# A decoder step on one core: the second half of layer 0's FFN by seven block products in 19 of its slices, with weight sums added by VectorE in place

## The chip, the cores and the metric

One Trainium2 chip; the program runs on one of its cores. The metric is the device time of one execution in microseconds (us), smaller is better. A core has engines with instruction streams of their own: TensorE (PE; its weight loads are listed apart as PEld and overlap the matmuls), VectorE (DVE), ScalarE (ACT), GpSimd (POOL) and SyncE (SP, which here only starts transfers). They wait for each other by semaphores. Working tiles lie in SBUF, matmul results in eight banks of PSUM, and the weights come from device memory (HBM) by DMA queues that the engines feed: SyncE's carries nearly all loads and stores, POOL's the transfers that add to what they write.

## The reference

One inference step of a decoder of two layers, in float32, for 1024 prompt tokens and 8 sample tokens. Every layer has a mixer (layer 0 a gated linear recurrence with memory attention, layer 1 stick-breaking attention over one shared K/V with memory attention) and then a feed-forward network, the FFN:

```python
D_MODEL = 1024
D_FF = ((8 * D_MODEL + 3 * 256 - 1) // (3 * 256)) * 256

def swiglu(h, w_gu, w_down):
    gate, up = jnp.split(h @ w_gu, 2, axis=-1)
    return (jax.nn.silu(gate) * up) @ w_down
...
    for l in range(DEPTH):
        g = g_norm[l]
        hn = rmsnorm(h, g[0])
        if l < N_A:
            mix, S = a_mixer(hn, w_in_a[l], lbs[l], hg_norm[l], mem_k[l], mem_v[l], w_o[l], hg_s0[l])
        else:
            mix = b_mixer(hn, w_in_b[l - N_A], sb_bias[l - N_A], k_all, v_all, q_pos, k_pos,
                          mem_k[l], mem_v[l], w_o[l])
        h = h + rmsnorm(mix, g[1])
        h = h + rmsnorm(swiglu(rmsnorm(h, g[2]), w_gu[l], w_down[l]), g[3])
```

D_FF is 2816, that is 22 slices of 128.

## The kernel before, in words

**Tokens and number format.** The tokens are worked on in two groups: g = 0 has 512 prompt tokens, g = 1 the other 512 and the 8 sample tokens, 520 columns in two halves of h = 260. Activations lie transposed, features on the partitions, eight tiles of 128 features. Every float32 operand is split in two parts in the format fp32r: ScalarE casts (the high part), VectorE subtracts the high part from the source (the low part). A product of two such operands is three matmuls: high by high, high by low, low by high. `split_w` (lines 206 and 207) does this for plain weights: raw weights come by a SyncE load into a buffer, the two parts go to a tile `ws`. `split_to` (227, 228) does it for activations.

**The FFN, three forms of it.** A slice is 128 of the 2816 middle features: its gate and its up projection, silu(gate) times up, and the split of the result into a middle tile `m`. The 22 slices go in five parts, `PARTS = [(0, 5), (5, 5), (10, 4), (14, 4), (18, 4)]` (first slice, count). After the slices of a part its down projection adds to the residual tile R: eight output tiles, nf x 3 x 2 matmuls each.
- class `ffn` (697) is the plain form: `proj` (212, matmul line 220) takes 8 tiles of features x 3 x 2 halves of columns = 48 matmuls for the gate, as many for the up projection, into PSUM pair tiles `mm`. Here silu is made of exponentials (`silu`, 230: clamp at -44 by VectorE, exp, ln, exp by ScalarE, a multiply by VectorE), the functions that attention needs too, so it can be interleaved with attention.
- `gate_up_q` (452) does the same 96 matmuls into four single banks Q(0) to Q(3), called `q`, and calls meanwhile for a share of the activations' block sums (the argument `side`). Its gate is ScalarE's Silu.
- `gate_up_w` (482) is the block form. Gate and up weights are a 2 x 2 block matrix (gate or up by rows 0-511 or 512-1023), the activations a 2 x 2 block matrix too (those rows by the two column halves). Seven products of blocks and sums of blocks give all four result blocks where eight would be used directly: `product` (505, matmul line 511) is 4 x 3 = 12 matmuls, a slice 84. Four of the products take sums of weight blocks, four take sums of activation blocks, `y`, `z` and `u`, made by `sums_w` (279), which adds the two halves of a split activation to the full value (`full`, four adds of 260 columns per pair of feature tiles, line 298) and then does four differences and their splits. A product's accumulator in part starts from the negated copy of another one: lines 518 and 521 are ScalarE copies by -1 from one bank to the next.

The order of a slice's products, with their accumulators, is written out by hand:

```python
        product(pa, 0, True)
        nc.scalar.activation(pb[:, :h], pa[:, :h], AF.Copy, scale=-1.0)
        product(pd, 1, True)
        product(pb, 2)
        nc.scalar.activation(pc[:, :h], pb[:, :h], AF.Copy, scale=-1.0)
        product(pa, 3)
...
        product(pb, 4)
...
        product(pc, 5)
...
        product(pb, 6)
        act[0] = nc.scalar.activation(sg[:, h:n], gt[:, :h], AF.Silu)
```

pa, pb, pc and pd are the banks q0 to q3. pa holds the gate, pb (after its last product) the up projection of the first half of the columns, and both are read by the next instructions before the next slice may write the bank again.

**Weight sums.** `weight_sums` (549) makes the four block sums of the weights in device memory: for each part 16 transfers on POOL's queue, copies (line 568) and adding transfers (566), half the rows at a time, each held back by a small copy (563) until the work has come as far as `now`. It is called for layer 0, parts 3, 4 and 2 (`w0`, 48 transfers) and for layer 1, all parts (`ws`, 80), and its steps are interleaved with other stages. `gate_up_w` then loads seven blocks for a slice, three from the weights and four sums (`weight`, 494).

**Class `ffn_w`** (575) drives `gate_up_q` and `gate_up_w` for some parts: the first slices are plain (as many as the list `steps` has, while the activations' sums are made), the others go by blocks. It also says where tiles are taken from: `spl` (593) split weights, from the pool `wspl` of five or a second pool `cpool`, `raws` (605) raw weights, YT the sums y, z and u.

**The order of the work.** There is one instruction stream per engine, in program order: the driver at the end of the function calls generators, and `weave` takes steps from several in given proportions. Around the change it does: heads of layer 1 for g = 0 (`b0.heads`); `b0.sb` (stick-breaking attention, 1340) and `b0.mem` (memory attention, 864) interleaved with parts 0 and 1 of layer 0's FFN for g = 1, in the plain form; then parts 2 to 4 by `ffn_w`, three plain and nine block slices; the output projection of b0 (`o0`), in small steps with finishing work; K/V and heads for g = 1; the plain FFN of layer 1 for g = 0 beside the second attention; and at the end layer 1's FFN for g = 1 by `ffn_w`, three plain and 19 block slices. The attention outputs go into eight split tiles `xo` (`wo_tiles`, 310), which stay in SBUF until `o0.mm` reads them, through all of parts 2 to 4; these tiles come from the pool of tag `x0`.

In layer 0's FFN for g = 1 thus nine of 22 slices go by blocks, 13 plain.

Of the kernel before, what the change touches and what calls it, by code (L numbers as in the profile page):

```python
# [18 lines left out]
P = 128  # L19
# [4 lines left out]
def tile_decoder(  # L24
# [204 lines left out]

    def silu(dst, ps, g):  # L230
# [48 lines left out]
    def sums_w(g, xs, ops, YT, ZT):  # L279
# [5 lines left out]
        for k in range(4):  # L285
# [15 lines left out]
            b11, b12, b21, b22 = full(x0, 0), full(x0, h), full(x1, 0), full(x1, h)  # L301
# [150 lines left out]
    def gate_up_q(g, l, f, xt, side, n_side, first):  # L452
# [4 lines left out]
        for j in range(2):  # L457
# [14 lines left out]
            for a in range(2):  # L472
                d = sg[:, a * h : (a + 1) * h]
                if j == 0:
# [7 lines left out]
    def gate_up_w(g, l, f, ops, spl, raws):  # L482
# [5 lines left out]
        src = [  # L488
            (w_gu[l][0:512, gate : gate + P], 0), (sums[l][part][0][:, o : o + P], 4), (sums[l][part][1][:, o : o + P], 5),
            (w_gu[l][512:D, gate : gate + P], 1), (sums[l][part][2][:, o : o + P], 6), (sums[l][part][3][:, o : o + P], 2),  # L490
            (w_gu[l][512:D, up : up + P], 3),
        ]

        def weight(j):
            r = raws()
            nc.sync.dma_start(r, src[j][0].rearrange("(k p) m -> p k m", p=P))
            return r.rearrange("p k m -> p (k m)")

        def split(src):
# [3 lines left out]
            return w  # L503

        def product(ps, j, first=False):
            w = split(weight(j))
            i = src[j][1]
# [16 lines left out]
        nc.scalar.activation(sg[:, :h], pa[:, :h], AF.Silu)  # L524
        product(pb, 4)
        dt = T()
        nc.scalar.copy(dt[:, h:n], pd[:, :h])
        gt = T()
        nc.vector.tensor_add(gt[:, h:n], dt[:, h:n], pb[:, :h])
        product(pc, 5)  # L530
        nc.vector.tensor_sub(gt[:, :h], pc[:, :h], dt[:, h:n])
        product(pb, 6)
        act[0] = nc.scalar.activation(sg[:, h:n], gt[:, :h], AF.Silu)
# [41 lines left out]
    class ffn_w:  # L575


        def __init__(self, g, l, x, steps, first, rows, R=None, own=False):
# [3 lines left out]
            self.half = []  # L582

            def YT():
                if rows:
# [5 lines left out]
            self.sums = sums_w(g, x, self.ops, YT, YT if rows else lambda: A(F32R))  # L591

        def spl(self):
            self.n += 1
            if (self.pi or not self.rows) and not self.own and self.n % 8 in (1, 4, 6):
# [9 lines left out]
        def raws(self):  # L605
            self.r += 1
            if not self.rows and self.r % 2:
# [1029 lines left out]
```

## Time and profile before

| | us |
|---|---|
| runs | 2447.81, 2451.44, 2450.1 |
| median | 2450.1 |
| the profiled execution's own time | 2446.43 |
| its span in the profile | 2444.6 |

The profile is that of one execution. Its span goes from the first to the last instruction; the execution's own time is 1.8 us more. The view by stretches of time (windows) gives for each stretch the busy time of each engine with its count of instructions; the view of groups gives a row for each line and shape: count, busy time, mean nanoseconds of one, and after the second bar the idle time just before them with what ended it ("<-ACT q L521 0.4": 0.4 us that a write to q by ScalarE at line 521 ended). A row of the waits gives who waits, for what, and the total, the count and the longest. In the timeline a row is the start, the duration, the engine, the line and the operation, and at its end how many instructions it merges. `out<-in` are the tiles by the program's names, so `ws<-w,ws` is a weight split, `q<-x,ws` a matmul.

The page's 40 slices of the span show TensorE at nine tenths or more in nearly all of them, and its granted clock at nine tenths or more throughout (0.999 on average).

Where the stages lie, by the lines in the timeline: attention of layer 1 for g = 0 woven with parts 0 and 1 of layer 0's second FFN from 990 to 1209 us, parts 2 to 4 of it to 1428, finishing, K/V and heads to 1530, layer 1's first attention and FFN half to 2085 and its last FFN to the end.

### The profile page before, as it was taken

Reading aid. Unit: us, or ns where it says so; the run is one execution under the profiler, and the core shown is the slowest. Engines: PE = TensorE matmul, PEld = TensorE weight load, DVE = VectorE, ACT = ScalarE, POOL = GpSimd, SP = SyncE. Lnnn points to the kernel's source line nnn. Section 1 sums busy time; section 2 is a strip of 40 time slices with the busy share of each in tenths; the row PEclk is TensorE's granted clock in tenths of the full one; section 3 lists DMA queues with packets and bytes.
Section 4 is the critical chain, followed back from the end, with each engine's and each line's share of the span. In section 5 each row is a group of like instructions: output and inputs, shape, how many; then the busy total and the mean of one; then the engine's idle time right before and its main releaser. Section 6 shows DMA issues by size and latency. Waiting matters only on the chain.

```text
span 2444.6 us, 42106 instructions
## 1 busy us (share of the span) xinstructions
PE 2412.0 (99%) x15839; PEld 2159.3 (88%) x15839; DVE 1639.0 (67%) x2987; ACT 1251.2 (51%) x2441; POOL 186.1 (8%) x315
## 2 busy tenths in 40 slices
PE   8999999999999999999999999999999999999998
PEld 6888888888889988999999989877777888999998
DVE  5867557665897686654756686777788467755565
ACT  5547544344445555554434554555555445654445
POOL 1001101101000000111200102121000100000000
PEclk9999999999999999999999999999999999999999
DMA  5454666577746447677766649655354563464542
GB/s 187 120 166 117 161 191 158 134 192 186 209 132 172 123 156 232 179 179 168 196 166 165 202 139 293 196 151 150 99 163 121 145 192 119 140 193 144 148 145 73
DMA packets 534734, 397.42 MB, mean 163 GB/s; under 512 B 21325, under 2 KB 473018, under 8 KB 534530
## 3 DMA queue, kind: packets, MB, share of 16 engines
q1 hardware_dynamic: 505346, 315.02, 43.3%
q0 software_dynamic: 29184, 79.70, 14.1%
q8 instruction: 125, 2.05, 0.3%
q14 instruction: 79, 0.65, 0.1%
HBM read 364.81 MB, written 101.14 MB: 191 GB/s over the span
## 4 chain that ended last, share of the span: by engine, by line
PE 87%; DVE 6%; DMA 3%; issue 2%; ACT 2%; POOL 0%; SPq 0%; DVEq 0%; ACTq 0%; POOLq 0%
PE mm L220 46%; PE q L511 13%; PE q L648 9%; PE q L464 3%; PE mm L1042 2%; PE s L1188 1%; PE s L906 1%; PE s L1385 1%; PE mm L851 1%; PE mm L824 1%; PE s L875 1%; PE q L680 1%; PE s L1351 1%; DVE ws L207 1%; DMA b<-qd 1%
## 5 line engine op out<-in xcount | busy, mean ns | idle before, releaser
L220 PE MATMUL mm<-x,ws 128*128 128x260 f32 (+1 forms) x6240 | 1115.6, 335 | 3.5 <-DVE r L657 1.7
L220 PEld LDWEIGHTS mm<-x,ws 128*128 128x128 f32 x6240 | 941.0, 188 | 123.9 <-DVE x L228 2.1
L206 ACT CAST ws<-w 128x512 fp32r<-128x512 f32 (+1 forms) x652 | 382.3, 588 | 492.1 <-PE mm L220 336.2
L207 DVE TENSOR_TENSOR ws<-w,ws 128x512 fp32r<-128x512 f32 (+1 forms) x652 | 418.6, 648 | 246.0 <-ACT ws L206 232.0
L220 PE MATMUL mm<-m,ws 128*128 128x512 f32 (+1 forms) x1344 | 281.8, 361 | 0.5 <-DVE r L400 0.4
L220 PEld LDWEIGHTS mm<-m,ws 128*128 128x128 f32 x1344 | 217.8, 188 | 37.2 <-issue 1.0
L648 PE MATMUL q<-m,ws 128*128 128x260 f32 (+1 forms) x1824 | 222.0, 282 | 0.0
L648 PEld LDWEIGHTS q<-m,ws 128*128 128x128 f32 x1824 | 219.0, 188 | 1.3 <-DVE t L534 0.7
L502 DVE TENSOR_TENSOR ws<-w,ws 128x512 fp32r<-128x512 f32 x181 | 124.0, 690 | 89.7 <-ACT ws L501 86.3
L501 ACT CAST ws<-w 128x512 fp32r<-128x512 f32 x181 | 111.8, 621 | 110.8 <-PE q L648 31.9
L511 PE MATMUL q<-x,ws 128*128 128x260 f32 (+1 forms) x1188 | 158.1, 282 | 0.0
L511 PEld LDWEIGHTS q<-x,ws 128*128 128x128 f32 x1188 | 148.7, 188 | 0.0
L511 PE MATMUL q<-y,ws 128*128 128x260 f32 x912 | 119.7, 283 | 0.4 <-ACT q L521 0.4
L511 PEld LDWEIGHTS q<-y,ws 128*128 128x128 f32 x912 | 113.6, 188 | 0.9 <-ACT q L521 0.6
L464 PE MATMUL q<-x,ws 128*128 128x260 f32 (+1 forms) x720 | 91.3, 284 | 0.2 <-DVE r L400 0.2
L464 PEld LDWEIGHTS q<-x,ws 128*128 128x128 f32 x720 | 88.4, 188 | 1.8 <-DVE r L400 0.5
L511 PE MATMUL q<-a,ws 128*128 128x260 f32 (+1 forms) x672 | 87.0, 282 | 0.0
L511 PEld LDWEIGHTS q<-a,ws 128*128 128x128 f32 x672 | 83.2, 188 | 0.0
L657 DVE TENSOR_TENSOR r<-r,q 128x260 f32<-128x260 f32 (+1 forms) x128 | 48.4, 420 | 48.2 <-PE q L648 48.1
L237 DVE TENSOR_SCALAR t<-mm 128x512 f32<-128x512 f32 (+1 forms) x58 | 40.0, 690 | 48.6 <-PE mm L220 48.4
L563 POOL COPY mk<-a 128x1 f32<-128x1 f32 x36 | 21.9, 609 | 640.4 <-ACT a L1241 392.1
L566 POOL DMA_DIRECT2D wsum<-in_w_gu x64 | 58.5, 935 | 114.1 <-DMA wsum<-wsum 89.5
(355 smaller groups left out, 3027.8 us busy)
## 6 DMA issues: line engine op xcount, KB each, us to landing
w<-in_w_gu SPq DMA_DIRECT2D x297, 256.0 KB
w<-in_w_down SPq DMA_DIRECT2D x160, 256.0 KB
wsum<-in_w_gu POOLq DMA_DIRECT2D x72, 512.0 KB, 6.5
w<-wsum SPq DMA_DIRECT2D x104, 256.0 KB
w<-in_w_in_a SPq DMA_DIRECT2D x80, 256.0 KB
w<-in_w_o SPq DMA_DIRECT2D x64, 256.0 KB
wsum<-in_w_gu POOLq DMA_DIRECT2D x24, 640.0 KB, 6.8
wsum<-wsum POOLq DMA_DIRECT2D x24, 512.0 KB, 5.6
```

The source lines that it names most:

```text
L206: nc.scalar.copy(ws[:, 0, :n, :], raw[:, :n, :])
L207: nc.vector.tensor_sub(ws[:, 1, :n, :], raw[:, :n, :], ws[:, 0, :n, :].bitcast(F32))
L220: nc.tensor.matmul(ps[:, a, : PW[g]], wt, xt[k][:, xi, o : o + PW[g]], start=(k == 0 and wi == 0), stop=(k == nk - 1 and wi == 2),)
L237: nc.vector.tensor_scalar(sv(x, g), pv(ps, g), -44.0, None, op0=ALU.max)
L464: ins = nc.tensor.matmul(pp[a][:, :h], wt, xt[k][:, xi, a * h : (a + 1) * h], start=(k == 0 and wi == 0), stop=(k == ND - 1 and wi == 2),)
L501: nc.scalar.copy(w[:, 0, :], src)
L502: nc.vector.tensor_sub(w[:, 1, :], src, w[:, 0, :].bitcast(F32))
L511: nc.tensor.matmul(ps[:, :h], w[:, wj, k * P : (k + 1) * P], x[:, xi, :], start=(first and k == 0 and wi == 0), stop=(k == 3 and wi == 2), ...
L566: nc.gpsimd.dma_start(d, a, accum_op=ALU.add)
L648: nc.tensor.matmul(pp[a][:, :h], wt, mids[k][:, xi, a * h : (a + 1) * h], start=(k == 0 and wi == 0), stop=(k == nf - 1 and wi == 2),)
L657: nc.vector.tensor_add(d, d, pp[a][:, :h])
L1042: nc.tensor.matmul(pb[i][:, a, :], xt[k][:, xi, c * P : (c + 1) * P], ws[:, s, :], start=(k == 0 and wi == 0), stop=(k == ND - 1 and wi == 2),
```

## The change

- **Layer 0's FFN for g = 1** now goes wholly through `ffn_w` with the lists `steps` from part 0 on: three plain slices (`gate_up_q`) and 19 block slices. Parts 0 and 1 (the argument `beside`) are those beside attention. The four PSUM banks q are set up before them (`set_banks(True)`).
- **The gate beside attention** (`lean`): in these parts `gate_up_q` and `gate_up_w` make silu of a clamp, exp, ln, exp and a multiply, for both column halves at once after the last product, where the others call Silu.
- **Weight sums in place**: a part without sums in memory (`ready` is None) loads its four raw blocks at the slice's start, and VectorE adds: one sum to a new tile of the pool `npool`, three in place over raw blocks that aren't needed any more, each just ahead of its cast. This holds for parts 0 and 1 of layer 0 (seven slices) and all of layer 1 (19). `weight_sums(1, ...)` and all its interleaved steps are gone; `w0` stays, for parts 2 to 4 of layer 0. Part 2's three plain slices become block slices.
- **Tiles**: in parts 0 and 1 raw blocks come in turns from two tiles of `cpool` (`spare`) and the raw pool, split weights from the five of `wspl` alone; the activations' sums lie in tiles of tag `x0`, where `xo` was. `sums_w` is given the unsplit activations (`src=o1.R`), so `full` isn't called.
- **The attention output of g = 0** goes to device memory (`open(True)`, `put`: a copy out of PSUM by ScalarE and a SyncE store for each of the eight) and comes back by `load`: four SyncE loads spread over part 2, and eight splits interleaved with part 4's down projection.
- **The driver** runs parts 2 and 3 one step after the other with these, no longer through `weave` with weight sums.

```diff
+    def put(xo, i, cols, src):
+        if isinstance(xo, list):
+            split_to((xo[i][:, 0, cols], xo[i][:, 1, cols]), src)
+            return
+        t = B()[:, : cols.stop - cols.start]
+        nc.scalar.copy(t, src)
+        nc.sync.dma_start(xo[:, i, cols], t)
...
-            b11, b12, b21, b22 = full(x0, 0), full(x0, h), full(x1, 0), full(x1, h)
+            if src:
+                b11, b12, b21, b22 = (src[i][:, c : c + h] for i in (k, k + 4) for c in (0, h))
+            else:
+                b11, b12, b21, b22 = full(x0, 0), full(x0, h), full(x1, 0), full(x1, h)
...
+    def gated(d, x):
+        nc.scalar.activation(d, x, AF.Exp, scale=-1.0)
+        nc.scalar.activation(d, d, AF.Ln, bias=1.0)
+        nc.scalar.activation(d, d, AF.Exp, scale=-1.0)
+        nc.vector.tensor_mul(d, d, x)
...
-    def gate_up_w(g, l, f, ops, spl, raws):
+    def gate_up_w(g, l, f, ops, spl, raws, lean=False):
...
+        ready = sums.get(l, {}).get(part)
+
+        def load(W):
+            r = raws()
+            nc.sync.dma_start(r, W.rearrange("(k p) m -> p k m", p=P))
+            return r.rearrange("p k m -> p (k m)")
...
+        raw = {}
+        if not ready:
+            raw = {"a11": load(block(0, gate)), "a21": load(block(0, up))}
+            raw.update(a22=load(block(512, up)), a12=load(block(512, gate)))
 
         def weight(j):
...
+            if j == 1:
+                s1 = N()[:, :512]
+                nc.vector.tensor_add(s1, raw["a21"], raw["a22"])
+                return s1
+            if j == 2:
+                nc.vector.tensor_add(raw["a21"], raw["a11"], raw["a21"])
+                nc.vector.tensor_add(raw["a11"], raw["a21"], raw["a22"])
+            if j == 5:
+                nc.vector.tensor_add(raw["a11"], raw["a11"], raw["a12"])
+            return raw[("a11", "", "a11", "a12", "a21", "a11", "a22")[j]]
...
         product(pb, 4)
         dt = T()
-        nc.scalar.copy(dt[:, h:n], pd[:, :h])
...
+        if lean:
+            gt = dt
+            nc.scalar.copy(dt[:, :h], pd[:, :h])
+            nc.vector.tensor_add(gt[:, h:n], dt[:, :h], pb[:, :h])
+            product(pc, 5)
+            nc.vector.tensor_sub(sg[:, h:n], pc[:, :h], dt[:, :h])
+            nc.vector.tensor_scalar(sg[:, h:n], sg[:, h:n], -44.0, None, op0=ALU.max)
+            x, sg = sg, T()
+            product(pb, 6)
+            gated(sg[:, :n], x[:, :n])
...
         def raws(self):
             self.r += 1
-            if not self.rows and self.r % 2:
+            if self.pi in self.beside and self.r % 9 < 4:
+                return self.spare[self.r % 9 // 2][:, self.r % 9 % 2].rearrange("p (k m) -> p k m", k=4)
...
+        def load(self):
+            d, n, self.xo = self.xo, NG[self.g], []
+            ts = []
+            for k in range(0, ND, 2):
+                t = A()
+                nc.sync.dma_start(t[:, :, :n], d[:, k : k + 2, :n])
+                ts += [t[:, 0, :n], t[:, 1, :n]]
+                yield
+            for t in ts:
+                x = X(self.g)
+                split_to((x[:, 0, :n], x[:, 1, :n]), t)
+                self.xo.append(x)
+                yield
...
-    ws = weight_sums(1, range(5))
...
-    b0.open()
+    weave((b0.heads(), 8), (o1.finish(), 17))
+    b0.open(True)
+    set_banks(True)
+    fw = ffn_w(1, 0, o1.x, (5, 6, 5), 0, False, beside=(0, 1), src=o1.R)
+    weave((chain(b0.sb(), b0.mem()), 25), (chain(fw.part(0), fw.part(1)), 18))
+    p4 = fw.part(4)
+    back = b0.load()
+    drain(fw.part(2), islice(back, 4))
+    drain(fw.part(3), islice(p4, 4))
+    weave((p4, 4), (back, 8))
     f1 = ffn(1, 0, o1.x)
-    weave((chain(b0.sb(), b0.mem()), 25), (chain(f1.part(0), f1.part(1)), 18), (islice(ws, 34), 35))
-    set_banks(True)
-    fw = ffn_w(1, 0, o1.x, (5, 6, 5), 2, False, f1.R)
-    weave((chain(fw.part(2), fw.part(3), fw.part(4)), 24), (islice(ws, 8), 8))
-    f1.acc = fw.acc
+    f1.R, f1.acc = fw.R, fw.acc
```

More of the change, by code (lines that the diff above doesn't have):

```diff
@@ L502, in split @@
             nc.vector.tensor_sub(w[:, 1, :], src, w[:, 0, :].bitcast(F32))
[L503 to L507, printed above, removed]
+            i = (0, 4, 5, 1, 6, 2, 3)[j]
             for k in range(4):
@@ L575, in tile_decoder, with __init__ @@
     class ffn_w:
-        def __init__(self, g, l, x, steps, first, rows, R=None, own=False):
+        def __init__(self, g, l, x, steps, first, rows, R=None, own=False, beside=(), src=None):
             self.g, self.l, self.x, self.ops, self.steps, self.rows, self.own = g, l, x, [], steps, rows, own
@@ L582, in __init__ @@
             self.half = []
+            self.beside = beside
+            self.spare = [C() for _ in beside[:2]]
             def YT():
-                if rows:
+                if rows or beside:
                     return xpool.tile([P, 2, NG[1]], F32R, tag="x0", name=nm("y"))
@@ L625, in part @@
                     mids.append(
-                        gate_up_q(g, l, f0 + j, self.x, self.sums, self.steps[j], PARTS[self.first][0])
+                        gate_up_q(
+                            g, l, f0 + j, self.x, self.sums, self.steps[j], PARTS[self.first][0], pi in self.beside
+                        )
                     )
```

77 lines of the change are left out of this document (43 added, 34 removed).

## The prediction, made before the changed kernel was run

> **What bounds the kernel now.** The page comes first: the busy line and the chain that ended last.
>
> ```profile
> PE 2412.0 (99%) x15839; PEld 2159.3 (88%) x15839; DVE 1639.0 (67%) x2987; ACT 1251.2 (51%) x2441; POOL 186.1 (8%) x315
> PE 87%; DVE 6%; DMA 3%; issue 2%; ACT 2%; POOL 0%; SPq 0%; DVEq 0%; ACTq 0%; POOLq 0%
> ```
>
> TensorE is hardly ever idle, and the chain is 87% TensorE. An average says little of the stages that the change touches, so next comes the view by stretches: 990 to 1209 us is attention of layer 1 woven with parts 0 and 1 of layer 0's second FFN, 1209 to 1428 is its parts 2 to 4, 2085 to 2420 is nearly all of layer 1's last FFN.
>
> ```profile
> core 0: us, PE busy (x) PEld busy (x) DVE busy (x) ACT busy (x) POOL busy (x), PEclk, DMA share, GB/s
> 990.00:1209.00 219.00, 218.35 (x1691) 207.96 (x1691) 133.26 (x262) 113.52 (x230) 34.56 (x65) 1.00 0.70 174
> 1209.00:1428.00 219.00, 218.10 (x1723) 212.95 (x1722) 131.74 (x240) 104.11 (x198) 18.71 (x27) 1.00 0.64 179
> 2085.00:2420.00 335.00, 334.36 (x2775) 332.01 (x2774) 204.46 (x391) 175.55 (x366) 0.00 (x0) 1.00 0.51 147
> ```
>
> In all three TensorE is busy but for about 1 us, at full clock, and VectorE is 60% busy. The waits of TensorE in the first and in the third stretch are one row each:
>
> ```profile
> PE s L1380 <- ACT b L1374: 0.3, 1, 0.3
> ```
>
> ```profile
> PE q L511 <- ACT q L521: 0.4, 1, 0.4
> ```
>
> So every matmul taken away is time taken away, as long as the other engines still deliver its neighbours in time. What a block product costs is seen in the timeline of TensorE: twelve matmuls, and the next product starts 1.44 us later.
>
> ```profile
> 2185.39 1.60 PE L511 MATMUL q<-x,ws 128*128 128x260 f32 x12
> 2186.83 1.61 PE L511 MATMUL q<-y,ws 128*128 128x260 f32 x12
> ...
> 2191.16 1.11 PE L511 MATMUL q<-x,ws 128*128 128x260 f32 x8
> ```
>
> From 2185.39 to 2191.16 are four products, 5.77 us, or 0.120 us for a matmul. The plain projections run at the same pace:
>
> ```profile
> 1183.98 25.20 PE L220 MATMUL mm<-m,ws 128*128 128x260 f32 x208
> ```
>
> 25.20 / 208 is 0.121 us.
>
> **The gain.** A plain slice has 2 x 8 x 3 x 2 = 96 matmuls of 260 columns, a block slice 7 x 12 = 84. Nine of 22 slices were block slices, nineteen will be: 10 x 12 = 120 matmuls fewer, 120 x 0.120 = **14.4 us**. 84 of them leave the woven stretch (7 slices), 36 part 2.
>
> **VectorE's new load.** The costs of one instruction:
>
> ```profile
> L502 DVE TENSOR_TENSOR ws<-w,ws 128x512 fp32r<-128x512 f32 x181 | 124.0, 690 | 89.7 <-ACT ws L501 86.3
> L946 DVE TENSOR_TENSOR c<-c 128x512 f32<-128x512 f32 x24 | 16.2, 684 | 0.1
> L531 DVE TENSOR_TENSOR t<-q,t 128x260 f32<-128x260 f32 (+1 forms) x33 | 14.1, 427 | 3.3 <-PE q L511 1.9 <-issue 0.6
> ```
>
> L946 is an in-place add of 512 columns, which is what the change adds: four for each of 7 + 19 slices, 104 in all. What counts in a queue is the pitch from start to start, and that is shorter than the 0.69 of busy time:
>
> ```profile
> 2105.15 0.68 DVE L502 TENSOR_TENSOR ws<-w,ws 128x512 fp32r<-128x512 f32 x1
> 2105.75 0.69 DVE L228 TENSOR_TENSOR m<-t,m 128x520 fp32r<-128x520 f32 x1
> 2106.36 2.49 DVE L502 TENSOR_TENSOR ws<-w,ws 128x512 fp32r<-128x512 f32 x4
> ```
>
> 0.60 and 0.61 from one to the next; for 260 columns I take 0.34, as 0.427 less the same overlap. The Trainium skill says otherwise (VectorE: DVE Perf Modes, The DRAIN you can't avoid): the next operation does not start until the pipeline has emptied. By it each would count with its full 0.69. The four subtractions in 2.49 us do not agree.
>
> A layer-1 slice then holds VectorE for 7 splits and 4 adds x 0.61, 4 combinations x 0.34 and one 0.61: 6.71 + 1.36 + 0.61 = 8.7 us, beside 84 x 0.120 = 10.1 us of TensorE. That fits, and the order of instructions keeps the splits one whole slice ahead of their matmuls, so I cost the 76 adds of layer 1 at nothing; if that cover goes, see the second rival. In the woven stretch: 133 + 28 adds (17) + 21 more splits (13) + about 6 for the new gate steps - 16 sums no longer rebuilt (5) - 8 attention splits moved away (5) = 159 of some 209 us. That fits too.
>
> **Weight sums through memory.** 80 of the 128 transfers of line 566 and 568 go, and 3 of 7 SyncE loads in each layer-1 slice.
>
> ```profile
> q0 software_dynamic: 29184, 79.70, 14.1%
> w<-wsum SPq DMA_DIRECT2D x104, 256.0 KB
> ```
>
> The only TensorE wait on a DMA in the stretch after them, 1530 to 1930, is small, so the relief is worth 0, at most 0.7 us:
>
> ```profile
> PE s L1351 <- DMA a<-ksc: 0.7, 1, 0.7
> ```
>
> **Late gate in the woven slices.** Here the gate is exp, ln, exp instead of one Silu, so the last product's accumulator (q1) is read later, and the next slice's third product must wait for it.
>
> ```profile
> L238 ACT ACTIVATE t<-t 128x512 f32<-128x512 f32 (+1 forms) x42 | 26.6, 634 | 24.9 <-DVE t L237 22.7
> L241 DVE TENSOR_TENSOR t<-t,t 128x512 f32<-128x512 f32 (+1 forms) x42 | 29.0, 691 | 36.6 <-ACT t L240 36.2 <-issue 0.3
> L518 ACT ACTIVATE q<-q 128x260 f32<-128x260 f32 (+1 forms) x33 | 12.2, 371 | 9.0 <-PE q L511 8.2
> L886 ACT ACTIVATE b<-s,nmx 128x256 f32<-128x256 f32 x64 | 29.8, 470 | 17.9 <-DVE nmx L880 17.8
> L886 ACT ACTIVATION_READ_ACCUMULATOR b<-s,nmx 128x1 f32 x64 | 12.6, 197 | 0.0
> L875 PE MATMUL s<-c,a 128*128 128x256 f32 x32 | 8.4, 379 | 0.0
> ```
>
> From the end of the sixth product: subtract 0.43, a split queued between (0.61), clamp 0.43; three ScalarE passes 1.90, in some slices with a cast between; multiply 0.69 and multiply by q1 0.43: 4.5 us. On ScalarE stand, before the negated copy that opens the third product, also two score exponentials (2 x 0.67) and a cast (0.62): 0.43 + 0.61 + 0.43 + 1.90 + 1.33 + 0.62 + 0.37 = 5.7 us, or 6.2 with the extra cast. Cover: products 7, 1 and 2, 3 x 1.44 = 4.33, and two score matmuls of 8.4 / 32 = 0.26: 4.9. The wait is 0.8 to 1.4 by busy times; by pitches (0.08 less on each of some seven) 0.3 to 0.8, and none where more attention matmuls lie between. I take 0.4 at each of five slice-to-slice changes, 2.0 (0 to 7). Behind that copy ScalarE holds the next casts, five buffers deep, so nothing else goes late. At the two changes to the down projection the last middle tile (two more steps, cast 0.62, subtract 0.69) comes about 6 us after, against 1.44 + 24 x 0.120 + 1 = 5.3: 0.8 each, 1.6 (0 to 4).
>
> **First block slice of layer 1.** VectorE arrives there already full:
>
> ```profile
> 2088.00:2100.00 12.00, 12.00 (x100) 11.73 (x100) 11.99 (x27) 5.67 (x13) 0.00 (x0) 1.00 0.38 112
> ```
>
> That is the view by stretches again (VectorE 11.99 of 12). From the timelines of VectorE and of TensorE, the first split and the second product's first matmuls:
>
> ```profile
> 2102.35 0.68 DVE L502 TENSOR_TENSOR ws<-w,ws 128x512 fp32r<-128x512 f32 x1
> ```
>
> ```profile
> 2104.69 0.41 PE L511 MATMUL q<-y,ws 128*128 128x260 f32 x2
> ```
>
> The second split starts at 2105.15 (quoted above), when TensorE is already at that product. Two adds now stand before it and three more before the third: 1.2 and 1.8 us later, with transposes as part cover. I take 2.5 (0 to 5).
>
> **Attention output by way of memory.** Eight stores, four reloads on SyncE's queue, and 8 casts and 8 splits behind the last block slice. A reload waits for its two stores, and behind it stand raw weight loads; nine raw buffers at four a slice reach 2.2 slices, 22 us, ahead, so the queue costs 0. The splits lie beside 8 x 24 x 0.120 = 23 us of down projection, but three stand before the last middle tile: 1.0 (0 to 2).
>
> **Sum.** -14.4 + 2.0 + 1.6 + 2.5 + 1.0 = -7.3 on the profiled execution's 2446.4 us (span 2444.6 and 1.8 around it): 2439.1. The median shown lies 3.7 above that execution, so 2450.1 - 7.3 = **2442.8**.
>
> **Rivals.** (1) All is covered: 2450.1 - 14.4 = 2435.7, 2435 with the DMA relief. For: hardly a wait of TensorE in any stretch; against: the 4.5 us gate chain. (2) **VectorE falls behind in layer 1**, slower: three of seven products now follow an add on their own tile, and VectorE, in order, waits out the cast (0.62) between add and subtraction. With full busy times 11 x 0.69 + 4 x 0.43 + 0.70 = 10.0, plus 3 x 0.62 = 11.9 against 10.1. It decides once pitch and waits pass 10.1 a slice. Halfway, at 11.2, 19 slices lose 21; at each of five parts the down projection gives VectorE time without splits, I take 2.3 us (an estimate: 24 x 0.120 less one subtract and its overlap, 0.61), which gives back 11; with the sum above, 2442.8 + 10, and more where the slack isn't had: about 2456, at worst 2465. For: the 86.3 us that L502 already waits on L501; against: the pitch, and a slice of lead. The skill's DRAIN rule would be on this side. (3) The waits eat the gain: 7 + 4 + 3 is 14 of 14.4, 2449.5. The Trainium skill has a rule that leans there (Perfetto Trace Analysis, Identifying the Most-Contended Engine): judge TensorE by LDWEIGHTS, not by matmul busy time. In the woven stretch that is 208 of 219, 95%, against 99% in layer 1; if matmuls there were worth nothing, 36 x 0.120 = 4.3 would be left, 2445.8 before any wait. The 0.3 us of waits speak against it.
>
> **How the numbers follow.** Forecast 0.36, its own range 2438 to 2447; rival 1 0.18; rival 2 0.26; rival 3 0.20. Below 0.2%, 4.9 us, a measurement here can't tell it from no change. Faster: rival 1 and most of the forecast, 0.51; same: the rest of it and rival 3, less what falls outside, 0.21; slower: rival 2 and a little of 3, 0.28. For 8 in 10 the range goes from 2433 (rival 1 with the relief, and 2 for the median of a few runs, which lie 2447.8 to 2451.4) to 2460.
>
> **What would show it.** 15719 matmuls instead of 15839, and the woven stretch with parts 2 to 4 some 10 us shorter than 438: right on the gain. TensorE waits on the negated copy (ACT q) in the woven slices, up to 1 us each: right on the gate. One wait of 2 to 3 us at the first block slice of layer 1. VectorE at 75% in layer 1's FFN with TensorE at 99%: right on the adds; TensorE waiting there in every slice on DVE ws makes the prediction wrong, as would a woven stretch as long as before.

## The result, and the profile after

| | before | changed |
|---|---|---|
| median of the first runs, us | 2448.95 (4 runs) | 2435.39 (4 runs, 2434.12 to 2437.57) |
| median when both were run again | 2448.37 (21 runs) | 2434.73 (5 runs) |
| ratio, 95% interval | | 0.9947 [0.9934, 0.9959]; again 0.9945 [0.9931, 0.9958] |
| the profiled execution's span | 2444.6 | 2435.9; in the second profile 2433.0 |

The change makes the kernel 13.6 us faster, by the second interval 10.3 to 16.9. The time lies in the stated range and almost on the figure of the first rival (2435.7, all is covered), outside the forecast's own 2438 to 2447. The profile has to say whether that rival's story is true as well. The page of the changed kernel, busy engines and the queue of the sum transfers:

```profile
PE 2400.0 (99%) x15719; PEld 2145.9 (88%) x15719; DVE 1720.7 (71%) x3152; ACT 1278.1 (52%) x2518; POOL 95.9 (4%) x155
...
q0 software_dynamic: 12544, 33.56, 5.8%
```

120 matmuls fewer, VectorE 82 us more, POOL's queue down from 79.7 MB to 33.6. Busy time says nothing of where the span shrank. For that both traces are cut at the same events: the first scores of layer 1's attention, the first matmul of part 2, the first of the output projection behind part 4, and the first plain matmul of layer 1's last FFN. In the kernel before, these lie at 990.74, 1209.13, 1404.93 and 2066.66 us: parts 2 to 4 end at 1404.93, and what follows up to 1428 is already the output projection. The view by stretches of the kernel before (columns as in the prediction; the second number is the stretch's length):

```profile
990.74:1209.13 218.39, 217.74 (x1689) 207.52 (x1688) 133.26 (x262) 113.52 (x230) 34.56 (x65) 1.00 0.70 174
1209.13:1404.93 195.80, 194.91 (x1622) 194.19 (x1621) 114.56 (x213) 91.40 (x176) 18.71 (x27) 1.00 0.67 187
1404.93:2066.66 661.73, 652.74 (x3518) 538.52 (x3519) 473.19 (x751) 338.31 (x622) 64.19 (x88) 1.00 0.56 162
2066.66:2444.62 377.96, 370.42 (x3075) 367.10 (x3073) 234.55 (x453) 202.11 (x421) 0.00 (x0) 0.99 0.48 139
```

And of the changed kernel, in its second profile:

```profile
990.29:1203.73 213.44, 208.79 (x1605) 197.97 (x1604) 157.97 (x327) 129.60 (x284) 0.00 (x0) 1.00 0.36 108
1203.73:1395.59 191.86, 191.01 (x1587) 190.31 (x1585) 123.88 (x231) 100.70 (x196) 8.48 (x8) 1.00 0.54 161
1395.59:2055.27 659.68, 652.80 (x3518) 539.28 (x3519) 473.53 (x751) 338.24 (x622) 26.14 (x24) 1.00 0.45 137
2055.27:2433.02 377.75, 370.43 (x3075) 366.68 (x3073) 278.03 (x528) 202.27 (x422) 0.00 (x0) 0.99 0.34 99
```

Row by row: the woven stretch (attention interleaved with parts 0 and 1) -4.95 us with 84 matmuls fewer; parts 2 to 4 -3.94 with 35 fewer in the records; the stretch in which not a matmul was changed, -2.05; the last FFN -0.2 with 75 more instructions on VectorE. With 0.45 us earlier at the start that is 11.6. In the woven stretch TensorE was idle 0.65 us before and is idle 4.65 us now. Its waits there in the changed kernel's first profile:

```profile
PE q L552 <- ACT q L559: 1.9, 4, 0.6
PE s L1411 <- DVE b L1424: 1.1, 1, 1.1
PE s L1445 <- ACT b L1442: 0.5, 1, 0.5
PE s L1440 <- ACT b L1434: 0.5, 1, 0.5
```

So not all is covered. The first row is the late gate. The wait of 1.1 us is in no term and no rival of the prediction: attention's score matmul waits for VectorE. Its timeline in the second profile, where the same wait was 1.29 us, shows why:

```profile
1087.95 0.69 DVE L534 TENSOR_TENSOR n<-w,w 128x512 f32<-128x512 f32 x1 [1.12 <-DMA w<-in_w_gu]
1088.68 0.69 DVE L537 TENSOR_TENSOR w<-w,w 128x512 f32<-128x512 f32 x1
1089.29 0.28 DVE L207 TENSOR_TENSOR ws<-w,ws 128x128 fp32r<-128x128 f32 x1
1089.49 0.35 DVE L1422 TENSOR_SCALAR b<-s,biasp 128x128 f32<-128x128 f32 x1
1089.75 0.34 DVE L1424 SCALAR_TENSOR_TENSOR b<-s,biasp,cap 128x128 f32<-128x128 f32 x1
```

L534 and L537 are two of the new adds, for the first slice of part 1 (L534 writes a new tile, L537 adds in place). The first of them waits for its raw block, and attention's two instructions, which set a score bank free, stand behind it.

### The profile page after: what moved, and what is told of

Its sections match the earlier page's. It is cut to its first block, busy times and chain, and to the rows that moved or that the text cites. A ratio compares the mean times of both kernels' runs of the same rounds, so it can differ in the third digit from the quotient of the medians.

```text
span 2435.9 us, 41748 instructions
## 1 busy us (share of the span) xinstructions
PE 2400.0 (99%) x15719; PEld 2145.9 (88%) x15719; DVE 1720.7 (71%) x3152; ACT 1278.1 (52%) x2518; POOL 95.9 (4%) x155
## 4 chain that ended last, share of the span: by engine, by line
PE 83%; DVE 8%; DMA 3%; ACT 3%; issue 3%; POOL 0%; SPq 0%; DVEq 0%; ACTq 0%; POOLq 0%
PE mm L220 39%; PE q L552 16%; PE q L709 11%; PE mm L1102 2%; PE q L481 2%; PE s L1248 1%; PE s L1445 1%; DVE ws L207 1%; PE s L967 1%; PE mm L885 1%; PE mm L912 1%; PE q L741 1%; DMA w<-in_w_gu 1%; DMA c<-in_cache_mem_v 1%; PE s L936 1%
## 5 line engine op out<-in xcount | busy, mean ns | idle before, releaser
L220 PE MATMUL mm<-x,ws 128*128 128x512 f32 (+1 forms) x5280 | 991.3, 344 | 4.4 <-DVE r L718 1.6
L220 PEld LDWEIGHTS mm<-x,ws 128*128 128x128 f32 x5280 | 823.5, 188 | 124.5 <-issue 2.7
L206 ACT CAST ws<-w 128x512 fp32r<-128x512 f32 x612 | 357.6, 586 | 459.1 <-PE mm L220 288.5
L207 DVE TENSOR_TENSOR ws<-w,ws 128x512 fp32r<-128x512 f32 x612 | 392.2, 646 | 238.5 <-ACT ws L206 226.1
L709 PE MATMUL q<-m,ws 128*128 128x260 f32 (+1 forms) x2304 | 284.0, 283 | 0.6 <-DVE m L228 0.6
L709 PEld LDWEIGHTS q<-m,ws 128*128 128x128 f32 x2304 | 277.7, 188 | 2.9 <-DVE t L589 1.0
L552 PE MATMUL q<-y,ws 128*128 128x260 f32 x1824 | 243.0, 284 | 2.3 <-ACT q L559 1.9
L552 PEld LDWEIGHTS q<-y,ws 128*128 128x128 f32 x1824 | 228.1, 188 | 3.9 <-ACT q L559 2.7
L220 PE MATMUL mm<-m,ws 128*128 128x512 f32 x864 | 219.7, 402 | 0.1
L546 ACT CAST ws<-w 128x512 fp32r<-128x512 f32 x188 | 115.7, 622 | 96.2 <-PE q L552 42.2
L547 DVE TENSOR_TENSOR ws<-w,ws 128x512 fp32r<-128x512 f32 x188 | 128.9, 689 | 50.2 <-ACT ws L546 47.9
L227 ACT CAST m<-t 128x512 fp32r<-128x512 f32 (+1 forms) x88 | 54.9, 623 | 22.6 <-DVE t L777 11.9
L228 DVE TENSOR_TENSOR m<-t,m 128x512 fp32r<-128x512 f32 (+1 forms) x88 | 60.8, 691 | 7.7 <-ACT m L227 7.4
L275 DVE TENSOR_TENSOR st<-st,n 128x512 f32<-128x512 f32 (+1 forms) x91 | 62.2, 691 | 2.1 <-ACT n L274 1.3
```

The source lines that it names most:

```text
L206: nc.scalar.copy(ws[:, 0, :n, :], raw[:, :n, :])
L207: nc.vector.tensor_sub(ws[:, 1, :n, :], raw[:, :n, :], ws[:, 0, :n, :].bitcast(F32))
L220: nc.tensor.matmul(ps[:, a, : PW[g]], wt, xt[k][:, xi, o : o + PW[g]], start=(k == 0 and wi == 0), stop=(k == nk - 1 and wi == 2),)
L227: nc.scalar.copy(dst[0], src)
L228: nc.vector.tensor_sub(dst[1], src, dst[0].bitcast(F32))
L275: nc.vector.tensor_add(acc[:, :n], acc[:, :n], t[:, :n])
```

## The experiments

"Us by spans" below is from one profiled execution, the median from several; where they differ by 2 us both are given.

**Both kernels again** (no edit).

> The changed kernel once more, for its time against before and for a second profile. Theory A: the profiles are right, the change is worth what its stages add up to there: -5.3 us in the woven stretch, -4.0 in parts 2 to 4, about -2 after it once the 1.7 us of the half-clock stretch at 1688 us is taken off, +0.9 ahead of it, some -10.5 us in all. Rival B: the medians are right, -13.6 us, and the second profile shows a woven stretch nearer to -10, the waits there having been chance. Expected: a ratio of 0.9945 to 0.996 by A, 0.994 to 0.995 by B; the waits on the negated copy are there again by A, 4 of about 0.5 us.

Measured: 2434.73 us, 0.9945 [0.9931, 0.9958]. The four waits on the negated copy were there again (2.1 us), and the woven stretch was 213.44 after 213.06. The interval holds both theories' ratios; the stretches are A's.

> The kernel before against itself: its ratio should be 1.000 within 0.001 by both theories. Its second profile says how far a stage moves from one execution to the next. If the start of the woven stretch (the first scores of layer 1's attention, 990.7 us in the first profile) moves by about 1 us, then the 0.9 us that the changed kernel came later there is scatter and no part of the change; if it stays within 0.3 us, the change has cost it.

Measured: 0.9999 [0.9990, 1.0008]. The woven stretch was 218.39 again and parts 2 to 4 195.57 after 195.80: these stretches hardly move from one execution to the next, and differences of half a microsecond can be read in them. The start of the woven stretch was 990.57 here, and 991.68 and 990.29 in the changed kernel's two profiles, so the 0.9 us was scatter. Like the first profile of the changed kernel this one has a stretch at half clock (last section). The stretch in which no matmul was changed does move: it was 664.55 us here after 661.73, and only 1.7 of the 2.8 are half clock; in the changed kernel it was 661.11 (1.7 of it half clock) and 659.68. Pairs with the same clock differ by 11.6 us (2444.6 and 2433.0) and 10.9 (2446.8 and 2435.9), the medians by 13.6. Where the other 2 us are was not settled; by this second profile of before that stretch alone gained some 3 us in place of 2, and the interval reaches down to 10.3.

**Layer 1's sums by transfers again, layer 0 as changed.**

```diff
+    ws = weight_sums(1, range(5))
...
-    weave((chain(b0.sb(), b0.mem()), 25), (chain(fw.part(0), fw.part(1)), 18))
+    weave((chain(b0.sb(), b0.mem()), 25), (chain(fw.part(0), fw.part(1)), 18), (islice(ws, 34), 35))
...
-    weave((p4, 4), (back, 8))
+    weave((p4, 4), (back, 8), (islice(ws, 8), 8))
```

The other 38 of the 80 steps stand where they did before.

> The changed kernel with layer 1's weight sums made in memory by POOL's transfers again, as before, and loaded ready; layer 0 as changed. Theory A: the 76 adds on VectorE cost nothing, and the 80 transfers cost TensorE about 2 us of waits between 1405 and 1650 us: this run is 1 to 2 us slower than the changed kernel, about 0.996 of before. Rival (VectorE limits layer 1's last FFN a little): this run is 1 us or more faster than the changed kernel, with the stretch from the first block product of layer 1 to the end about 1 us shorter.

Measured: 2471.32 us, 1.0094 [1.0078, 1.0109]. Both theories fell: without the in-place sums of layer 1, the change to layer 0 makes the kernel 0.9% slower than before. The woven stretch, as a row of the view by stretches, and its first waits:

```profile
990.59:1226.09 235.50, 212.50 (x1605) 200.81 (x1604) 155.89 (x325) 129.14 (x284) 37.85 (x67) 0.97 0.73 186
```

```profile
PE s L1445 <- ACT b L1442: 7.2, 4, 3.4
PE q L552 <- DVE r L718: 6.1, 1, 6.1
PE s L1411 <- DVE b L1424: 5.3, 1, 5.3
```

22 us more than with the transfers gone, at a mean clock of 0.97 (the third number from the right). The engines named are not the cause; ScalarE's and VectorE's timelines show what they had waited for:

```profile
1223.67 0.62 ACT L546 CAST ws<-w 128x512 fp32r<-128x512 f32 x1 [9.44 <-DMA w<-in_w_gu]
```

```profile
1100.41 0.69 DVE L534 TENSOR_TENSOR n<-w,w 128x512 f32<-128x512 f32 x1 [5.10 <-DMA w<-in_w_gu]
```

It is the same add ahead of attention as above, with 5.10 us of waiting for its raw block in place of 1.12. Where they stood in the kernel before, beside plain slices of the same parts, the same 34 transfers cost nothing, as the next run shows.

**The kernel before with layer 1's adds alone.** `gate_up_w` as changed, `ws` and its steps taken out of the driver, the rest as before. Layer 1's raw blocks come in turns from two pools in part 0 too, where the kernel before used one; the second pool is another than in the changed kernel.

> The kernel before with only layer 1's weight sums moved to VectorE (four adds a slice, in place) and the 80 transfers gone; layer 0 as before. Theory A: 0 to -2 us against before (0.999 to 1.000). Rival: slower by 1 us or more (1.0005 and above). With the run before it, it says whether the two halves of the change add up.

Measured: 2445.56 us, 0.9987 [0.9978, 0.9996]. The woven stretch is 218.38, as with the transfers. The stretch up to the last FFN and the last FFN itself:

```profile
1405.56:2065.53 659.97, 652.41 (x3519) 538.55 (x3520) 473.71 (x751) 338.36 (x622) 26.14 (x24) 1.00 0.46 139
2065.53:2444.58 379.05, 371.08 (x3075) 367.34 (x3073) 277.95 (x528) 202.19 (x422) 0.00 (x0) 1.00 0.32 96
```

-1.8 us and +1.1 us against before. The 2 us that the changed kernel gains where no matmul was changed thus come from the transfers that are gone. The two halves of the change do not add: -2.8 us for this one by medians, +23 for the other, -13.6 together.

**The gate in halves.** The first half's gate is computed ahead of the sixth product, and the bank q1 is read right behind the last one:

```diff
+            x, sg = sg, T()
+            nc.vector.tensor_scalar(x[:, :h], pa[:, :h], -44.0, None, op0=ALU.max)
...
             nc.scalar.copy(dt[:, :h], pd[:, :h])
+            gated(sg[:, :h], x[:, :h])
...
             product(pb, 6)
-            gated(sg[:, :n], x[:, :n])
+            nc.vector.tensor_mul(sg[:, :h], sg[:, :h], pb[:, :h])
+            gated(sg[:, h:n], x[:, h:n])
```

> The changed kernel with the gate beside attention made in two halves: the first column half's exp, ln, exp and multiply stand ahead of the sixth product, and the last product's bank (q1) is read right behind that product, ahead of the second half's gate. Nothing is left out. Theory A (the wait on the negated copy comes from the gate's chain): the four waits, 2.0 us in all and some 2.7 us by the starts of the products, go, and the woven stretch, 213.1 and 213.4 us in the two profiles so far, becomes 210.5; some 0.9935 of before. Rival (ScalarE's queue, which gets three more instructions a slice, is what makes attention and products wait): the waits move to the scores and the stretch stays at 213 or grows.

Measured: 2432.99 us, 0.9933 [0.9920, 0.9947], the fastest of the runs that leave no sum out; its interval overlaps with that of the changed kernel. The row of the stretch:

```profile
992.27:1203.44 211.17, 208.31 (x1605) 197.81 (x1604) 157.28 (x334) 132.70 (x305) 0.00 (x0) 1.00 0.36 108
```

2.1 us shorter than the mean of the changed kernel's two, and no wait on the negated copy is left. The gate's chain has a part in that wait (theory A); the run without adds below shows that it isn't alone in it.

**The gate made longer.** In the lean branch of `gate_up_w`, ahead of `gated`:

```diff
+            for _ in range(2):
+                nc.scalar.activation(x[:, :n], x[:, :n], AF.Copy)
```

> The changed kernel with two more ScalarE passes over the 520 columns ahead of the exp in the gate of block slices beside attention; values unchanged. Theory A: each of five slice-to-slice changes waits 1.1 to 1.3 us longer, the two changes to the down projection up to as much, and the woven stretch goes from 213.3 to 219 to 222 us. Rival (the wait is set by something else): less than 2 us longer.

Measured: 2444.92 us, 0.9983 [0.9973, 0.9993]; the stretch 225.02 us at a mean clock of 0.98, that is about 220.5 at full clock (225.02 x 0.98, an estimate). The profile is that of the slowest of eight executions, 2450.85 us. The length is A's, the place is not: over the woven stretch and parts 2 to 4 the waits were

```profile
PE s L962 <- DVE b L955: 3.1, 3, 1.1
PE s L1442 <- ACT b L1436: 2.3, 3, 1.6
PE q L552 <- ACT q L559: 1.8, 2, 1.3
PE s L1447 <- ACT b L1444: 1.6, 2, 1.0
```

A longer gate is paid for mostly by attention's matmuls, whose ScalarE and VectorE steps stand behind it in the same queues.

**VectorE's slack in layer 1.** Each add accompanied by one more instruction of its size:

```diff
+                if l:
+                    nc.vector.tensor_tensor(s1, s1, s1, op=ALU.max)
                 return s1
```

and likewise for the three others.

> The changed kernel with every add of layer 1's weight sums accompanied by one more VectorE instruction of the same size on the same tile (a maximum of a tile with itself; values unchanged): 76 more. Theory A (VectorE has little slack in a block slice: 8.7 us of 10.1 by starts, 11.1 with these): it falls behind in the slices and recovers in the down projections, 5 to 12 us slower than the changed kernel, with TensorE waiting on VectorE's splits in the later slices of a part. Rival (the slack is larger than reckoned): under 2 us slower.

Measured: 2438.62 us, 0.9958 [0.9943, 0.9973]: 3.9 us slower than the changed kernel by medians, 3.6 by spans; between the two theories. The last FFN:

```profile
2056.28:2436.56 380.28, 371.57 (x3075) 367.05 (x3073) 316.46 (x604) 200.03 (x422) 0.00 (x0) 0.99 0.33 99
```

It is 2.5 us longer than 377.75, with VectorE at 316 of 380 us, and 2.1 of them are in part 0: its down projection starts 63.01 us after the stretch's first matmul, against 60.87 in the changed kernel. Of TensorE's waits there only the first block slices show one that matters:

```profile
PE q L560 <- ACT q L567: 1.6, 1, 1.6
```

No later slice waits for a split, so the queue of ready splits was never used up there.

**No adds in layer 1.** `weight` returns a raw block in place of each sum for layer 1.

> The changed kernel with layer 1's weight sums left out: the products take a raw block in place of each sum, so the 76 adds are gone and the output of layer 1 is another. Theory A: the adds cost next to nothing; the stretch from layer 1's first plain product to the last down projection, 341.8 and 341.3 us against 340.9 and 340.7 before, goes back to about 340.7, and the whole is 0 to 1 us faster than the changed kernel. Rival (the adds are paid for by waits that no row names): 2 us or more faster.

Measured: 2434.39 us, 0.9942 [0.9927, 0.9957]; by medians the changed kernel's time, by spans 1.8 us less, and the last FFN is

```profile
2054.98:2431.17 376.19, 369.53 (x3075) 366.48 (x3073) 235.41 (x454) 202.35 (x420) 0.00 (x0) 1.00 0.33 100
```

1.6 us below 377.75 (2.0 below the 378.20 of the first profile). The 76 adds cost 1.6 to 2.0 us, more than A said. By the starts of the down projections and of the parts behind them, 0.2 of the 1.6 lie in part 0, where the first block slice is, 0.9 in the five slices of part 1 and 0.5 in part 3's down projection. Without the adds the FFN is 1.8 us faster than before, and the number of loads is not the reason: in the run with layer 1's sums by transfers a slice has seven loads as before, and the same stretch took

```profile
2086.95:2463.50 376.55, 369.51 (x3075) 366.47 (x3073) 235.22 (x454) 202.05 (x420) 0.00 (x0) 0.99 0.48 139
```

**The transfers moved out of the woven stretch.** As two runs further up, with `(islice(ws, 34), 35)` in the `weave` of layer 1's first attention.

> As l1_by_dma (layer 0 as changed, layer 1's weight sums made by POOL's transfers), but the 34 steps of those transfers that stood in the woven stretch of layer 0 now stand in layer 1's first attention, woven with plain slices, where no block slice loads. Theory A (the transfers are dear only where in-place block slices load beside attention: 17 of the 20 us lost in l1_by_dma, with its half-clock stretches, lie in the woven stretch): the woven stretch is back at 213 to 214 us without waits on loads, and the whole is 2436 to 2445 us. Rival (the transfers are dear wherever they stand): still 2455 or more.

Measured: 2468.45 us, 1.0083 [1.0068, 1.0099]. The woven stretch is A's, 212.53 us without a wait on a load. The total is the rival's. From the output projection to the scores of the next attention 159.30 us passed where the kernel before took 148.67, with the DMA engines at 0.85, and TensorE's first waits there are

```profile
PE s L1411 <- DMA a<-ksc: 5.0, 1, 5.0
PE s L1375 <- ACT t L1370: 5.0, 2, 4.8
```

In both runs the eight steps that lay beside parts 2 to 4 before came bunched at the end of part 4, and these waits may be the price of that bunch; it was not tried apart. The larger loss lies behind them, in the attention with plain slices beside which the 34 transfers now stand. From its first scores to the last FFN, before and in this run:

```profile
1553.60:2066.66 513.06, 506.72 (x2506) 404.44 (x2507) 367.32 (x576) 262.24 (x488) 40.05 (x52) 1.00 0.50 145
1556.90:2090.47 533.57, 514.73 (x2507) 409.91 (x2507) 367.45 (x576) 261.38 (x487) 80.76 (x120) 0.98 0.63 173
```

That is 20.5 us more, where no block slice loads: the transfers are dear not only beside block slices, as A said. VectorE waits there for the loads of the sample tokens' queries:

```profile
DVE c L993 <- DMA b<-qd: 20.1, 10, 4.0
```

In the kernel before the same waits came to 2.2 us. Attention's steps stand behind them in VectorE's queue: after three of the longest, which ended at 1637.77, 1650.04 and 1787.98 us, TensorE waited 1.9, 2.9 and 3.7 us for VectorE and ScalarE. The attention of the woven stretch, beside which the transfers were free, has no sample tokens.

**No adds in layer 0's woven parts.** As for layer 1, for parts 0 and 1 of layer 0.

> The changed kernel with the 28 adds of weight sums in parts 0 and 1 of layer 0 left out: the products take a raw block in place of each sum, so the output is another. Theory A (the adds stand in VectorE's queue ahead of attention's steps on the score bank, and one of them waits for a load): the wait of the scores on VectorE at about 1090 us, 1.1 to 1.3 us in three profiles of the changed kernel, goes, and the woven stretch becomes 211 to 212 instead of 213.1 and 213.4. Rival (attention waits there because the products are fewer, whatever VectorE does): that wait and the stretch stay.

Measured: 2432.40 us (2 runs), 0.9936 [0.9918, 0.9954]. The stretch:

```profile
991.74:1201.32 209.58, 208.44 (x1605) 197.95 (x1604) 141.94 (x300) 130.05 (x283) 0.00 (x0) 1.00 0.36 108
```

3.5 to 3.9 us shorter, better than expected: the scores' wait at 1090 us is gone, and so is the wait on the negated copy, which A had not said. That wait thus needs both, the gate's chain and the adds. In the changed kernel's second profile ScalarE idled for an add, and the gate's first pass came behind (in the first profile the same idle time, 1.99 us, is put down to a matmul):

```profile
1113.16 1.14 ACT L546 CAST ws<-w 128x512 fp32r<-128x512 f32 x2 [2.20 <-DVE w L538]
1114.74 0.64 ACT L464 ACTIVATE t<-t 128x520 f32<-128x520 f32 x1 [0.44 <-DVE t L577]
```

**All sums on VectorE, on top of the gate in halves.** `w0` and its steps taken out.

> The gate in halves, and in addition the weight sums of layer 0's parts 2, 3 and 4 made by VectorE too, for both groups: no transfers on POOL's queue for sums are left. Theory A (a transfer taken away relieves TensorE where it stood, and the block slices of parts 2 to 4 have VectorE to spare): up to 2 us faster than the gate in halves alone, 2430 to 2433. Rival (parts 3 and 4 of the first group run beside attention with raw tiles from a pool that attention uses): 2 us or more slower, with waits of attention or of the products in the stretch before 750 us.

Measured: 2437.64 us, 0.9956 [0.9942, 0.9969], 4.6 us slower than the gate in halves by medians, 2.8 by spans. The stretch before, which the rival named, is not longer beyond scatter (the woven stretch starts at 992.45, with the gate in halves at 992.27). Parts 2 to 4 take 193.81 us against 191.88, and the relief that A hoped for does not show. Both were wrong about the place.

**Two of four adds on GpSimd, on top of the gate in halves.**

```diff
-                nc.vector.tensor_add(s1, raw["a21"], raw["a22"])
+                (nc.vector if l else nc.gpsimd).tensor_add(s1, raw["a21"], raw["a22"])
```

and the next add likewise.

> The gate in halves, and in parts 0 and 1 of layer 0 the first two of a slice's four adds made by GpSimd, which has nothing to do there; the other two stay on VectorE. Theory A (without its 28 adds the woven stretch was 209.6 us against 213.1 and 213.4, so VectorE's queue is what is left of the loss there): with 14 adds off VectorE the stretch becomes 209.5 to 210.5 instead of 211.2, and the whole is about 1 us faster than the gate in halves alone, some 2432. Rival (an add of 512 columns takes GpSimd several times the 0.69 us of VectorE, for which no row of this case has a price, and the second and third product wait for it, or VectorE's own instructions beside it get longer): the stretch becomes 213 us or more.

Measured: 2438.71 us, 0.9964 [0.9951, 0.9978]; the woven stretch is 216.00. The rival is right. Groups of GpSimd, and of VectorE's splits beside them:

```profile
L537 POOL TENSOR_TENSOR w<-w,w 128x512 f32<-128x512 f32 x3 | 4.2, 1392 | 0.2
...
L534 POOL TENSOR_TENSOR n<-c,c 128x512 f32<-128x512 f32 x1 | 2.1, 2069 | 21.9 <-DVE b L1434 21.9
```

```profile
L547 DVE TENSOR_TENSOR ws<-c,ws 128x512 fp32r<-128x512 f32 x19 | 14.5, 762 | 4.9 <-ACT ws L546 4.8
```

An add takes GpSimd 1.3 to 2.1 us by its groups in this stretch, and 19 of VectorE's splits have gone from 688 to 762 ns in the mean. The Trainium skill (GPSIMD Engine Reference, 4.1 Engine selection) puts elementwise work with two inputs at about twice VectorE's time there; 1392 against 690 ns agrees; the add of 2069 ns took three times as long.

## Why the prediction was right or wrong

The sign and the range were right; the sum, -7.3, was 4 us short of what the spans give (-11.6) and 6 short of the medians. Its base, 2450.1, was the median of three executions and 1.7 above the later one of 21; on that one the forecast would have been 2441.1 and the first rival 2434.0. By its own steps:

- **The gain, -14.4.** 15719 matmuls, as said. The share of parts 2 to 4 was 4.3 and came nearly whole (-3.9). Of the 10.1 in the woven stretch 8.8 came in the run without adds there (218.39 to 209.58), 5.0 to 5.3 in the changed kernel.
- **Late gate, +2.0.** Right in place and number: four waits of 0.5 us on the negated copy, 1.9 and 2.1 in all; with the gate in halves they are gone and 2.1 us with them. The mechanism was half of it, and the size is in part luck: the working left out the adds, which hold back the casts that stand ahead of the gate's passes, and in the run without adds the gate's chain alone makes no such wait.
- **Two changes to the down projection, +1.6.** Wrong: the matmuls of L709 show no wait in the woven stretch.
- **VectorE in the woven stretch, costed at nothing.** This step failed on the bad side. The count, 159 of 209 us, was right (158), but an engine with a quarter of its time free still works in order. The 28 adds and what waits behind them cost 3.5 to 3.9 us, some 2 of which are the gate's wait.
- **First block slice of layer 1, +2.5, and the other adds there at 0.** The mechanism was misplaced. TensorE has only small waits there (its own transposes lie between the products), 0.2 us of loss, while the 76 adds together cost 1.6 to 2.0, most of it in the part behind. Only with twice the adds did 2.1 us come at the first part. The last FFN still came out at -0.2 and +0.2: without the adds it is 1.8 faster than before. Why is open: it is not the loads, since with seven a slice it was 1.4 faster too. Part 0's raw blocks also come from another choice of tiles than before, which was not tried apart.
- **Reload of the attention output, +1.0.** Some 0.4 (4.3 less 3.9), or 0.7 if the 0.3 that parts 2 to 4 gained from the missing transfers alone (195.50 after 195.80) is added.
- **Relief from the transfers, 0, at most 0.7.** This term was mis-sized most: 2.05 us by the spans (some 3 by the second profiles), 1.8 in the run that took nothing else out of this stretch. The bound came from the one wait named DMA, that of L1351 on `ksc`, 0.7 and 1.0 us in the two profiles of before and 0.2 to 0.4 or none without the transfers. But waits on ScalarE went too: those of the matmuls of L1315 from 0.6 and 1.2 us to 0.2, and those of L1380 (L1440 in the changed kernel) from 2.1 and 1.6 to 1.1 and 1.0. With L1385 (L1445), 1.9 and 2.9 before and 2.1 and 1.9 after, the four rows come to 5.3 and 6.7 us before and 3.7 and 3.3 after, which is about the relief.
- **Rivals.** The time is the first one's, its condition does not hold: TensorE's idle time in the woven stretch rose by 4 us, and the relief and 2 us not settled filled the gap. The second, VectorE falling behind in layer 1, did not happen, and not even with 76 more instructions there beyond a few us. (Its price was also too high by its own figures: halfway between 10.0 and 11.9 is 10.95, not 11.2; 19 slices then lose 16 us, 5 after what the down projections give back, and the time is some 2448.) The third, waits that eat the gain, came true by half in the woven stretch (5 of 10.1) and nowhere else.

What the prediction did not see at all is that the two halves hang together: it costed the transfers by the trace of a stage in which they were free, and the change put block slices there, beside which the same transfers cost 22 us. Block slices are not the only such place: beside the sample tokens' attention and plain slices the 34 transfers came with a loss of 20.5. Common to both is an engine that waits, in order, for a load; that this is the whole reason was not tried apart.

## What to carry to other kernels

When a change makes a stage's loads more urgent, what else uses the DMA engines there must be priced against the new stage: a transfer that is free in one stage can be the bound in another, and moving it to a third that looks free can cost as much again. Free time on an in-order engine is not cover for an instruction that waits for a load; see what stands behind it, and read a bank that others wait for before a long gate, not after it. Two parts of a change can be worth -2.8 and +23 us alone and -13.6 together, so try each part alone before crediting either.

## What the runs showed of the hardware

A wait of TensorE can cost more than its length. In the changed kernel's first profile TensorE waited 1.92 us up to 1675.99; the granted clock (the third number from the right) in the microseconds after it:

```profile
1676.00:1677.00 1.00, 1.00 (x9) 1.00 (x9) 0.50 (x2) 0.98 (x2) 0.00 (x0) 1.00 0.99 329
...
1678.00:1679.00 1.00, 1.00 (x4) 0.60 (x3) 0.97 (x2) 0.33 (x1) 0.36 (x1) 0.50 0.01 4
...
1681.00:1682.00 1.00, 1.00 (x6) 0.80 (x5) 0.00 (x0) 0.00 (x0) 0.04 (x1) 1.00 0.84 285
```

With 0.64 and 0.65 in the first and the last of the slow microseconds and 0.50 in the two between, that is some 3.4 us at half clock, 1.7 us lost. In the second profile the same wait was 1.94 us long, and the clock stayed at 1.00. In the second profile of the kernel before a wait of 2.34 us at this place was followed by the same (0.63, 0.50, 0.50 and 0.66 in the microseconds from 1687 on). In the run with layer 1's sums by transfers the clock was at half during the end of the wait of 5.26 us and for some 3.6 us after it. The Trainium skill (TensorE: Matmul & The Clock Gate, HAM oscillation — how this bites in real kernels) has the clock fall after idle gaps of more than about 3.4 us; here it fell after shorter ones, and after one of 1.94 us it did not. No run was made to find the bound.
